# Attention scores of a two-layer trunk in fp32 pieces: the low query against both heads' high keys, the high query against high and low keys stacked in the rows, with halves moved between partitions by DMA

## The chip, the cores and the metric

The kernel runs on one core of one Trainium2 chip, in one launch. The metric is the device time of that launch in microseconds (us): 609.42 us, the median of 3 runs (609.11 to 610.04).

## What is computed

Two layers, each one RMSNorm, one wide input projection (1024 to 9808 columns, for 256 positions), three causal attention mixers of 8 heads of 64 (plain "a", indexer-selected "b", forgetting "c"), a SiLU gate per mixer, a projection per mixer, merge gates, an output projection and the residual; then one last norm. What the change touches is every product of queries and keys: the scores of the three mixers and those of the indexer.

```python
s_own = jnp.einsum('bhqd,bhkd->bhqk', qc, k_own).astype(jnp.float32) * scale      # a
rel = jax.nn.relu(jnp.einsum('bqhd,bsd->bqhs', qi, k_idx))                        # indexer: 8 query heads, one key
s = jnp.einsum('bqhd,bkhd->bhqk', qc, k)                                          # b and c, in chunks
p = jax.nn.softmax(s, axis=-1)
```

The 256 positions are one block of a, so a is plain causal attention. The indexer keeps 64 keys per query for b.

## The kernel before

**Numbers in two pieces.** TensorE multiplies `float32r` operands. To keep fp32 accuracy each fp32 operand X is split: ACT writes the high piece Xh (a copy rounded to `float32r`), DVE writes the low piece Xl = X - Xh. A product is then three matmuls that add up in one PSUM bank: high x high, low x high, high x low. Every weight goes through this: 1 MB or 0.5 MB chunks are loaded by the queue of SyncE (SP) into three `raw` buffers (L354), split by ACT into `wh` (L362) and by DVE into `wl` (L366), and multiplied (L410, all units of projections).

**Work units.** The PE's work is a list of units. A unit of the input projection (`unit_b`, L422) makes 128 output columns for all 256 positions: 24 matmuls of 256 moving columns. Units `q`, `k`, `g` of a pair of heads (128 rows = 2 heads of 64) make its query, key and gate; `m` units make merge gates, `y` units (12 matmuls) the projections of a finished mixer. `mixer` (L986) lists the units of a mixer, two pairs of heads at a time, in the order q, g, k; `between` (L997) puts m and y units among them as filling. `NB1` says how many of the merge-gate units of mixer b stand there and how many stand behind mixer b (L1040, L1042).

**The planner.** No engine's order is written by hand. Every step is given to `Plan.op` with its engine, an estimated cost, what it reads and writes, and a key (its unit's number, shifted). `Plan.run` (L138) then lists the steps: at each turn the engine that can start first takes, of its steps that are ready then, the one with the lowest key. Each engine, SP's queue among them, executes its list strictly in order. A step of SP that waits for its source so holds the loads listed behind it.

**Queries.** `ev_q` (L594): for a and b the projection is rotated first (`rope`, L461: DVE shuffle, POOL multiply, DVE multiply, POOL add; result `rr` in SBUF), for c it is read from PSUM. `split_to` (L390) writes `qh` by ACT and `ql` by DVE, 128 x 256 each; the rows are the two heads.

**Keys.** `ev_k` (L603) calls `write_bd` (L721). The key of the pair is stored block-diagonally, so that one matmul with all 128 rows serves both heads: tile `bd..h` is 128 x (2 x 256), head 0's key in the upper rows of the first half, head 1's in the lower rows of the second half, zeros elsewhere (written once, L912 to L919). `bd..l` is the same for the low piece. Per key that is two ACT copies (L727) and two DVE subtractions (L728), each on 64 rows. The indexer's one key (`ev_kwf`, L732) is written to both diagonal blocks.

**Scores.** `scores` (L574) is one step on PE. The queries are the stationary operand (128 positions at a time), the block-diagonal keys move: for the first 128 queries 2 x 128 key columns (only the causal part), for the second 128 queries 2 x 256.

```python
PE.matmul(o, qh[:, sl], mh, start=True, stop=False)     # L584
PE.matmul(o, ql[:, sl], mh, start=False, stop=False)    # L585
PE.matmul(o, qh[:, sl], ml, start=False, stop=True)     # L586
```

That is six matmuls per call: 3 of 256 columns and 3 of 512. `scores` is called 16 times per layer (12 pairs of the mixers by `attend`, L637; 4 pairs of the indexer by `index_scores`, L785), 32 times in all. The two heads' scores lie interleaved in PSUM (column, head), which the readers undo by a stride of 2 (L647, L797). After the scores come, per head and half: bias and row minimum (DVE, L647), exponential (ACT, L651), normalising, transposes (PE, L673), the split of the result (L676, L678) and the product with the values (PE, L690 to L693).

Of the kernel before, what the change touches and what calls it, by code (L numbers as in the profile page):

```python
# [47 lines left out]
NB1 = 0  # L48
# [186 lines left out]
def hybrid_trunk(ctx, tc, x, norm_gain, w_in, forget_bias, w_branch, w_out, final_gain, consts, out):  # L235
# [15 lines left out]
    def T(b):  # L251
        return b.slot[1]
# [29 lines left out]
    qs = [[pool.tile([128, S], F32R, name=f"q{p}{i}") for i in range(3)] for p in "hl"]  # L282
# [8 lines left out]
    bd = [[pool.tile([128, 2, S], F32R, name=f"bd{i}{p}") for p in "hl"] for i in range(NBD)]  # L291
# [41 lines left out]
    for nm, n, cols, dt in (("rsh", 2, S, F32), ("rr", 2, S, F32),  # L333
                            ("th", 2, S, F32), ("g", 4, S, F32), ("e", 4, 384, F32), ("st", 8, 8, F32),
                            ("fb", 2, 384, F32), ("ot", 2, S, F32), ("t8", 4, 8, F32), ("mth", MTH, S, F32)):
        tag(nm, n, [128, cols], dt)
# [134 lines left out]
    def new_bd():  # L471

        b = Buf("bd")
        return b, [[Tok(), Tok()], [Tok(), Tok()]]


# [97 lines left out]
    def scores(q, k, ktoks, key):  # L574
        s0, s1 = Buf("s"), Buf("s")
        kt = [t for h in ktoks for t in h]

        def go():
            qh, ql = T(q[0]), T(q[1])
            kh, kl = T(k)  # L580
            for o, sl, n in ((T(s0)[:, :256], slice(0, 128), 128), (T(s1), slice(128, 256), 256)):
                o = o.rearrange("p (c h) -> p c h", h=2)
                mh, ml = (x[:, :, :n].rearrange("p h c -> p c h") for x in (kh, kl))
                PE.matmul(o, qh[:, sl], mh, start=True, stop=False)  # L584
                PE.matmul(o, ql[:, sl], mh, start=False, stop=False)  # L585
                PE.matmul(o, qh[:, sl], ml, start=False, stop=True)  # L586
        pe(go, 3 * (t_mm(256) + t_mm(512)), [q[0], q[1], k] + kt, [s0, s1], key, "qk", MARGIN)
        return s0, s1

    class Pair:  # L590
# [3 lines left out]
        def ev_q(self, ps, key):  # L594
            q = self.q = (Buf("qh"), Buf("ql"))
            if self.mixer == "c":
                split_to(lambda: plain(T(q[0])), lambda: plain(T(q[1])), lambda: tiles(T(ps)[:, :S]), S, True, [ps], q[0], q[1],
                         key, -0.125, "q")
            else:
                r = rope(ps, "q", key)  # L600
                split_to(lambda: plain(T(q[0])), lambda: plain(T(q[1])), lambda: tiles(T(r)), S, False, [r], q[0], q[1], key, name="q")

        def ev_k(self, ps, key):  # L603
            self.k, self.kt = new_bd()
            src = ps if self.mixer == "c" else rope(ps, "k", key)
            write_bd(src, self.k, self.kt, key, self.mixer == "c")
# [30 lines left out]
        def attend(self, key):  # L637
# [3 lines left out]
            for h in range(2):  # L641
# [4 lines left out]
                for t, a, n, s in parts:  # L646
                    dve(lambda t=t, a=a, n=n, s=s, e=e, st=st, b=b, h=h: DVE.tensor_tensor_reduce(  # L647
                        T(e)[:, a:a + n], T(s)[:, :2 * n].rearrange("p (c h) -> p h c", h=2)[:, h], b()[:, a:a + n], 1.0, 3e38, ALU.add, ALU.min,
# [72 lines left out]
    def write_bd(src, b, toks, key, ps, shared=False):  # L721
        for h in range(2):
            o = slice(64 * h, 64 * h + 64)
            s = (lambda: tiles(T(src)[0:64, :S])) if shared else (lambda o=o: tiles(T(src)[o, :S]))
            hi = lambda o=o, h=h: plain(T(b)[0][o, h])
            lo = lambda o=o, h=h: plain(T(b)[1][o, h])
            act(lambda hi=hi, s=s: ACT.activation(hi(), s(), AF.Copy), S, ps, [src, k_bdz], [toks[h][0]], key, "bd", HALF + (0.0 if ps else 104.0), touch=[b])  # L727
            dve(lambda hi=hi, lo=lo, s=s: DVE.tensor_tensor(lo(), s(), hi().bitcast(F32), op=ALU.subtract), S,  # L728
                [src, toks[h][0]], [toks[h][1]], key, "bd", t_dve(S) + HALF + 15.0, touch=[b], port=not ps)


    def ev_kwf(l, ps, key):  # L732
        act(lambda: ACT.activation(plain(wf[64:80]), tiles(T(ps)[64:80, :S]), AF.Copy), S, True, [ps], [k_wf], key, "wf")
        b, toks = new_bd()
        write_bd(rope(ps, "k", key, 64), b, toks, key, False, shared=True)
        return b, toks
# [357 lines left out]
```

## Time and profile before

| | |
|---|---|
| median of 3 runs | 609.42 us |
| the profiled execution's own time | 609.16 us |
| its span, first to last instruction | 607.4 us |
| granted TensorE clock | 0.997 |
| DVE busy | 537.9 us (89%) |
| ACT busy | 406.8 us (67%) |
| POOL busy | 85.7 us (14%) |
| bytes moved by DMA | 105.55 MB, mean 174 GB/s |

A matmul's row gives its start and the time until its end, and matmuls overlap: the next one starts before the last has drained. How long PE is held by a matmul is therefore read from the distance between starts, not from the duration. PEld is the load of a stationary operand; it runs beside the matmul before it. In the timeline a row is: start, duration, engine, line, operation, out<-in, stationary rows*columns, moving rows x columns, count. In rows of one source line, three numbers with slashes are the shortest, median and longest duration in ns. An idle time in brackets names what ended it.

### The profile page before, as it was taken

The numbers are of one execution on the slowest core, as the hardware profiler recorded it, in microseconds if no ns is written. First come the engines' busy times: TensorE is split into PE (matmuls) and PEld (weight loads), VectorE is DVE, ScalarE is ACT, GpSimd is POOL, SyncE is SP. The second block draws the span as 40 slices with busy tenths as digits, with TensorE's granted clock in tenths as the row PEclk, the third lists the DMA queues.
The fourth block names the chain that finished last, engine by engine and source line by source line (L and its number), as shares of the span: only waits on it lengthen the run. The fifth ranks groups of instructions, "written<-read, shape, count | busy, mean of one in ns | idle before, by whom it ended". The sixth has DMA issues, their size and how long they took to land.

```text
span 607.4 us, 12561 instructions
## 1 busy us (share of the span) xinstructions
PE 599.1 (99%) x4856; PEld 580.8 (96%) x4856; DVE 537.9 (89%) x1270; ACT 406.8 (67%) x811; POOL 85.7 (14%) x100
## 2 busy tenths in 40 slices
PE   9999999999999999999999999999999999999995
PEld 8999999999999999999889999999999999999995
DVE  8799999887998999999588899978889989999883
ACT  6775487685776766785587554957767675859741
POOL 1224021100000222200003311201000004230001
PEclk9999999999999999999999999999999999999998
DMA  9866455837372562666555637474464437355801
GB/s 304 255 209 208 127 169 157 278 104 231 117 245 70 159 203 92 209 211 206 161 181 169 206 102 246 139 219 142 153 187 174 141 115 224 109 182 164 280 35 70
DMA packets 93853, 105.55 MB, mean 174 GB/s; under 512 B 4321, under 2 KB 82401, under 8 KB 93793
## 3 DMA queue, kind: packets, MB, share of 16 engines
q1 hardware_dynamic: 93504, 104.36, 53.8%
q8 instruction: 38, 0.62, 0.4%
q10 hardware_dynamic: 288, 0.39, 0.2%
q14 instruction: 23, 0.18, 0.1%
HBM read 103.69 MB, written 1.05 MB: 172 GB/s over the span
## 4 chain that ended last, share of the span: by engine, by line
PE 88%; DVE 9%; issue 1%; ACT 1%; DMA 0%; POOL 0%; POOLq 0%; DVEq 0%
PE proj L410 74%; DVE wl L366 3%; PE t L673 3%; PE proj L970 2%; PE s L586 2%; PE s L585 2%; PE s L584 2%; PE o L690 1%; PE o L693 1%; DVE isc L824 1%; DVE t L823 1%; PE t L629 1%; DVE isc L803 1%; DVE rsh L465 1%; PE o L692 0%
## 5 line engine op out<-in xcount | busy, mean ns | idle before, releaser
L366 DVE TENSOR_TENSOR wl<-raw,wh 128x1024 fp32r<-128x1024 f32 (+1 forms) x190 | 237.1, 1257 | 24.2 <-ACT wh L362 22.6
L362 ACT ACTIVATE wh<-raw 128x1024 fp32r<-128x1024 f32 (+1 forms) x190 | 198.6, 1058 | 74.3 <-PE proj L410 43.1
L410 PE MATMUL proj<-hTh,wh 128*128 128x256 f32 (+1 forms) x1040 | 246.4, 276 | 0.0
L410 PE MATMUL proj<-hTl,wh 128*128 128x256 f32 (+1 forms) x1040 | 245.6, 275 | 0.0
L410 PEld LDWEIGHTS proj<-hTl,wh 128*128 128x128 f32 (+1 forms) x1040 | 199.0, 191 | 0.4
L410 PEld LDWEIGHTS proj<-hTh,wh 128*128 128x128 f32 (+1 forms) x1040 | 198.9, 191 | 0.4
L410 PE MATMUL proj<-hTh,wl 128*128 128x256 f32 (+1 forms) x1040 | 160.1, 276 | 0.0
L410 PEld LDWEIGHTS proj<-hTh,wl 128*128 128x128 f32 (+1 forms) x1040 | 138.0, 191 | 0.9
L466 POOL TENSOR_TENSOR rsh<-rsh,cst 128x256 f32<-128x256 f32 (+1 forms) x42 | 33.0, 786 | 343.0 <-DVE rsh L465 333.9
L651 ACT ACTIVATE e<-e,st 128x128 f32<-128x128 f32 x96 | 42.6, 446 | 9.2 <-DVE st L647 8.9
L468 POOL TENSOR_TENSOR rr<-rr,rsh 128x256 f32<-128x256 f32 (+1 forms) x42 | 44.4, 1059 | 9.7 <-ACT wh L362 3.4
L410 PE MATMUL proj<-wh,v 128*128 128x512 f32 (+1 forms) x144 | 33.7, 356 | 0.0
L410 PE MATMUL proj<-og0l,wh 128*128 128x256 f32 x128 | 31.9, 275 | 0.0
L410 PE MATMUL proj<-og0h,wh 128*128 128x256 f32 x128 | 31.9, 275 | 0.0
L410 PE MATMUL proj<-wh,hTh 128*128 128x512 f32 x80 | 31.4, 393 | 0.0
L410 PE MATMUL proj<-wh,hTl 128*128 128x512 f32 x80 | 30.5, 382 | 0.2 <-DVE hTl L532 0.2
L706 ACT ACTIVATE ot<-o 64x256 f32<-64x256 f32 x48 | 18.3, 381 | 16.8 <-PE o L693 16.3
L410 PEld LDWEIGHTS proj<-wh,v 128*128 128x128 f32 x144 | 25.2, 190 | 2.9
L678 DVE TENSOR_TENSOR ptl<-t,pth 128x384 fp32r<-128x384 f32 x48 | 25.1, 551 | 0.2
L410 PE MATMUL proj<-og0h,wl 128*128 128x256 f32 x128 | 24.7, 275 | 0.0
L410 PEld LDWEIGHTS proj<-og0h,wh 128*128 128x128 f32 x128 | 24.6, 192 | 0.0
L410 PEld LDWEIGHTS proj<-og0l,wh 128*128 128x128 f32 x128 | 24.6, 192 | 0.0
(194 smaller groups left out, 1012.3 us busy)
## 6 DMA issues: line engine op xcount, KB each, us to landing
raw<-in_w_in_dram SPq DMA_DIRECT2D x74, 1024.0 KB, 5.2
raw<-in_w_branch_dram SPq DMA_DIRECT2D x24, 512.0 KB, 3.9
raw<-in_w_out_dram SPq DMA_DIRECT2D x8, 1024.0 KB, 5.5
raw<-in_w_in_dram SPq DMA_DIRECT2D x3, 512.0 KB, 6.3
x<-in_x_dram SPq DMA_DIRECT2D x4, 256.0 KB, 4.1
raw<-in_w_in_dram SPq DMA_DIRECT2D x2, 320.0 KB, 6.7
out_dram<-tmp SPq DMA_DIRECT2D x2, 320.0 KB, 2.5
raw<-in_w_in_dram SPq DMA_DIRECT2D x2, 256.0 KB, 3.4
```

The costliest lines, as they stand in the source:

```text
L362: ACT.activation(p[0].v, sel(c.v), AF.Copy)
L366: DVE.tensor_tensor(p[1].v, sel(c.v), p[0].v.bitcast(F32), op=ALU.subtract)
L410: PE.matmul(o(), a(), b(), start=first and i == 0, stop=last and i == n - 1)
L466: gps(lambda: POOL.tensor_tensor(T(sh)[:np_], T(sh)[:np_], s[:np_], op=ALU.mult), S, [k_rope], [sh], key, "rope")
L468: gps(lambda: POOL.tensor_tensor(T(r)[:np_], T(r)[:np_], T(sh)[:np_], op=ALU.add), S, [sh], [r], key, "rope")
L584: PE.matmul(o, qh[:, sl], mh, start=True, stop=False)
L585: PE.matmul(o, ql[:, sl], mh, start=False, stop=False)
L586: PE.matmul(o, qh[:, sl], ml, start=False, stop=True)
L651: act(lambda t=t, a=a, n=n, e=e, st=st: ACT.activation(T(e)[:, a:a + n], T(e)[:, a:a + n], AF.Exp, bias=T(st)[:, t:t + 1], scale=-1.0, acc ...
L673: PE.transpose(T(ps)[:, i * 128:(i + 1) * 128], T(es[h])[:, i * 128:(i + 1) * 128], ident)
L678: dve(lambda h=h, src=src: DVE.tensor_tensor(T(pl)[:, h], src(), T(ph)[:, h].bitcast(F32), op=ALU.subtract), 384, [ps, kp[h][0]], [kp[h][1 ...
L706: act(lambda r=r, h=h: ACT.activation(T(t)[r], T(o)[64:, h * S:(h + 1) * S], AF.Copy, scale=0.5), S, True, [o], [kt[h]], key, "og", HALF, ...
```

## The change

- **The products.** The block-diagonal tile now holds only the high key (`bd..h`). A second tile, `bd..e`, holds for each head the high key in that head's own 64 rows and the low key in the other 64 rows. The query's high piece is kept per head, once in the upper and once in the lower rows (`qh` is now 128 x (2 x 256)). One matmul of low query x block-diagonal high key serves both heads as before; then one matmul per head, with all 128 rows, adds high query x (high key + low key). Per half of the queries that is one matmul of 2n moving columns and two of n, in place of three of 2n (n = 128, 256). The half with n = 256 comes first.
- **The pieces.** ACT writes the high query and the high key twice side by side (512 columns in one instruction, reading the source twice). DVE makes the low query and the low key in one subtraction each on all 128 rows; the low key goes to a buffer `kl` of its own.
- **The moves.** What must change partitions goes by DMA on SP's queue (`move`, a new step): two transfers per query, four per key in two steps, each 64 rows x 256 columns (64 KB). A move is planned as 0.8 us of SP and landed 1.9 us later. The indexer's one key needs none: its two ACT copies, a third ACT copy and one DVE subtraction write all blocks.
- **Layout.** The scores of the two heads lie one behind the other in PSUM, no longer interleaved; the readers are changed to match.
- **Order.** `mixer` lists q, k, g in place of q, g, k. `NB1` is 2 in place of 0: two of the eight merge-gate units of mixer b stand among its pairs, six behind. There are 3 buffers `rr` in place of 2. Three zeroed tiles fall away. A smaller scratch area for DMA descriptors is asked for.

```diff
-NB1 = 0
+NB1 = 2
-    qs = [[pool.tile([128, S], F32R, name=f"q{p}{i}") for i in range(3)] for p in "hl"]
+    qs = [[pool.tile([128, 2, S] if p == "h" else [128, S], F32R, name=f"q{p}{i}") for i in range(3)] for p in "hl"]
+    klow = [pool.tile([128, S], F32R, name=f"kl{i}") for i in range(2)]
...
+    def move(dst, src, n, reads, writes, key, name, touch=()):
+
+        def go():
+            for d, a in zip(dst(), src()):
+                nc.sync.dma_start(d.bitcast(F32), a.bitcast(F32))
+        o = plan.op([("SP", 800.0, go)], reads, writes, key, 1900.0, name, touch)
+        o.margin = -1350.0
...
-            for o, sl, n in ((T(s0)[:, :256], slice(0, 128), 128), (T(s1), slice(128, 256), 256)):
-                o = o.rearrange("p (c h) -> p c h", h=2)
-                mh, ml = (x[:, :, :n].rearrange("p h c -> p c h") for x in (kh, kl))
-                PE.matmul(o, qh[:, sl], mh, start=True, stop=False)
-                PE.matmul(o, ql[:, sl], mh, start=False, stop=False)
-                PE.matmul(o, qh[:, sl], ml, start=False, stop=True)
+            for o, sl, n in ((T(s1), slice(128, 256), 256), (T(s0)[:, :256], slice(0, 128), 128)):
+                both = kh[:, :, :n].rearrange("p h (a b) -> p h b a", a=2)
+                PE.matmul(o.rearrange("p (h b a) -> p h b a", h=2, a=2), ql[:, sl], both, start=True, stop=False,
+                          skip_group_check=True)
+                for h in range(2):
+                    oh = o[:, h * n:(h + 1) * n].rearrange("p (b a) -> p b a", a=2)
+                    PE.matmul(oh, qh[:, h, sl], turns(ke[:, 0 if shared else h, :n]), start=False, stop=True,
+                              skip_group_check=True)
...
+    def split_q(q, src, ps, b, key, scale, name):
...
+        act(lambda: ACT.activation(T(q[0]).rearrange("p h (a b) -> p h a b", a=2), two(src()), AF.Copy, **sc), 2 * S, ps,
+            [b], [k], key, name, 0.0 if ps else 144.0, touch=[q[0]])
...
+        lo, up = slice(0, 64), slice(64, 128)
+        move(lambda: (T(q[0])[up, 0], T(q[0])[lo, 1]), lambda: (T(q[0])[lo, 0], T(q[0])[up, 1]), S, [], [q[0], k], key - 6, "dq")
...
+    def split_k(src, ps, key):
+        b, kl = Buf("bd"), Buf("klow")
...
+        act(lambda: ACT.activation(T(b)[1].rearrange("p h (a b) -> p h a b", a=2),
+                                   sv().unsqueeze(1).to_broadcast([128, 2, 2, 128]), AF.Copy), 2 * S, ps,
+            [src], [ka], key, "bd", 0.0 if ps else 144.0, touch=[b])
+        dve(lambda: DVE.tensor_tensor(plain(T(kl)), sv(), plain(T(b)[1][:, 0]).bitcast(F32), op=ALU.subtract), S,
+            [src, ka], [kl], key, "bd", t_dve(S) + (10.0 if ps else 26.0), touch=[b], port=not ps)
+        move(lambda: (T(b)[0][LO, 0], T(b)[0][UP, 1]), lambda: (T(b)[1][LO, 0], T(b)[1][UP, 1]), S, [ka, k_bdz], [k0],
+             key - 6, "dk", [b])
+        move(lambda: (T(b)[1][UP, 0], T(b)[1][LO, 1]), lambda: (T(kl)[LO], T(kl)[UP]), S, [kl], [ka, k1], key - 6, "dk", [b])
+        return b, [ka, k0, k1]
...
-                for hf in range(2) for kind in "qgk" for p in (2 * hf, 2 * hf + 1)]
+                for hf in range(2) for kind in "qkg" for p in (2 * hf, 2 * hf + 1)]
```

On PE, the scores of the first pair of mixer c in layer 0 stand so before (`s` are the two banks of scores, `bd2h` and `bd2l` the keys, `qh` and `ql` the queries, `proj` the unit around them):

```order
L410 MATMUL proj_158<-hTl,wh_68 128x256
L584 MATMUL s_159<-bd2h,qh_82 128x256
L585 MATMUL s_159<-bd2h,ql_85 128x256
L586 MATMUL s_159<-bd2l,qh_82 128x256
L584 MATMUL s_160<-bd2h,qh_82 128x512
L585 MATMUL s_160<-bd2h,ql_85 128x512
L586 MATMUL s_160<-bd2l,qh_82 128x512
L410 MATMUL proj_158<-hTh,wl_75 128x256 x4
```

The unit around them is the next pair's key (kc1). After the change the same scores stand as follows; the unit around them is now the next pair's gate (gc1), one key unit, two y units and one gate unit later:

```order
L412 MATMUL proj_160<-hTh,wl_74 128x256 x4
L586 MATMUL s_163<-bd2h,ql_85 128x512
L590 MATMUL s_163<-bd2e,qh_82 128x256 x2
L586 MATMUL s_162<-bd2h,ql_85 128x256
L590 MATMUL s_162<-bd2e,qh_82 128x128 x2
L412 MATMUL proj_160<-hTh,wh_68 128x256
```

There are still six matmuls. Between the last matmul of the key unit kc0 and these scores stand 20 matmuls of 256 columns and 4 small ones before, and 84 of 256 columns and 4 small ones now. Counted so for each of the 32 calls, from the last matmul of its query or key unit, the PE work in between is now least for the third pair of mixer c (kc2): 60 matmuls of 256 columns, 8 of the product with the values, 3 transposes and 4 small ones (20 and 4 small ones before).

On SP's queue, around the loads for the same stretch of mixer c in layer 0, there stand before only loads (`raw` are the three load buffers):

```order
L354 DMA raw_117<-in_w_in_dram 128x8x256
L354 DMA raw_115<-in_w_in_dram 128x8x256
L354 DMA raw_116<-in_w_branch_dram 128x4x256
L354 DMA raw_117<-in_w_in_dram 128x8x256
L354 DMA raw_115<-in_w_branch_dram 128x4x256
```

Now moves stand between them (`qh` a query's halves; `bd..h<-bd..e` the high key to the block-diagonal tile; `bd..e<-kl` the low key to the stacked tile; kc0's are those with `bd2`, kc1's those with `bd0`):

```order
L574 DMA qh_82<-qh_82 64x256 x2
L356 DMA raw_117<-in_w_in_dram 128x8x256
L574 DMA qh_80<-qh_80 64x256 x2
L574 DMA bd2h<-bd2e 64x256 x2
L356 DMA raw_118<-in_w_branch_dram 128x4x256
L574 DMA bd0h<-bd0e 64x256 x2
L574 DMA bd2e<-kl_86 64x256 x2
L356 DMA raw_119<-in_w_in_dram 128x8x256
L574 DMA bd0e<-kl_87 64x256 x2
```

Each load now has moves listed ahead of it and behind it. In all, SP's list grows from 124 transfers to 284: 160 moves, 64 for queries and 96 for keys.

More of the change, by code (lines that the diff above doesn't have):

```diff
@@ L290, in hybrid_trunk @@
     NBD = 3
-    bd = [[pool.tile([128, 2, S], F32R, name=f"bd{i}{p}") for p in "hl"] for i in range(NBD)]
+    bd = [[pool.tile([128, 2, S], F32R, name=f"bd{i}{p}") for p in "he"] for i in range(NBD)]
     pts = [pool.tile([128, 2, 384], F32R, name=f"pt{p}") for p in "hl"]
@@ L571, in final_norm, with scores @@
         plan.op([("SP", 50.0, lambda: nc.sync.dma_start(out_rows[:, B], tmp6[:, B]))], [ko[1], k_tmp[1]], [], key, 1900.0, "out")
-    def scores(q, k, ktoks, key):
+    def move(dst, src, n, reads, writes, key, name, touch=()):
[4 more added lines that the diff above has]
+        o.margin = -1350.0
+    def scores(q, k, ktoks, key, shared=False):
@@ new lines, in scores @@
+        pe(go, 775.0, [q[0], q[1], k] + ktoks, [s0, s1], key, "qk", MARGIN)
+        return s0, s1
+    def split_q(q, src, ps, b, key, scale, name):
+        k = Tok()
+        two = lambda x: x.unsqueeze(1).to_broadcast([128, 2, 2, 128])
+        sc = {} if scale is None else {"scale": scale}
+        act(lambda: ACT.activation(T(q[0]).rearrange("p h (a b) -> p h a b", a=2), two(src()), AF.Copy, **sc), 2 * S, ps,
+            [b], [k], key, name, 0.0 if ps else 144.0, touch=[q[0]])
+        hi = lambda: plain(T(q[0])[:, 0]).bitcast(F32)
+        if scale is None:
+            f = lambda: DVE.tensor_tensor(plain(T(q[1])), src(), hi(), op=ALU.subtract)
+        else:
+            f = lambda: DVE.scalar_tensor_tensor(plain(T(q[1])), src(), scale, hi(), op0=ALU.mult, op1=ALU.subtract)
+        dve(f, S, [b, k], [q[1]], key, name, t_dve(S) + (10.0 if ps else 26.0), touch=[q[0]], port=not ps)
+        lo, up = slice(0, 64), slice(64, 128)
+        move(lambda: (T(q[0])[up, 0], T(q[0])[lo, 1]), lambda: (T(q[0])[lo, 0], T(q[0])[up, 1]), S, [], [q[0], k], key - 6, "dq")
@@ L719, in gated @@
                      k_og[self.oi][0][self.p], k_og[self.oi][1][self.p], key, name="og")
[L721 to L729, printed above, removed]
+    LO, UP = slice(0, 64), slice(64, 128)
@@ L732, in ev_kwf @@
     def ev_kwf(l, ps, key):
         act(lambda: ACT.activation(plain(wf[64:80]), tiles(T(ps)[64:80, :S]), AF.Copy), S, True, [ps], [k_wf], key, "wf")
-        b, toks = new_bd()
-        write_bd(rope(ps, "k", key, 64), b, toks, key, False, shared=True)
-        return b, toks
+        r, b = rope(ps, "k", key, 64), Buf("bd")
+        ka, k0, k1 = Tok(), Tok(), Tok()
+        sv = lambda: tiles(T(r)[LO, :S])
+        for o, h, k in ((LO, 0, k0), (UP, 1, k1)):
+            act(lambda o=o, h=h: ACT.activation(plain(T(b)[0][o, h]), sv(), AF.Copy), S, False, [r, k_bdz], [k], key, "bd",
+                HALF + 104.0, touch=[b])
@@ L738, in wf_cols @@
+        act(lambda: ACT.activation(plain(T(b)[1][LO, 0]), sv(), AF.Copy), S, False, [r], [ka], key, "bd", HALF + 104.0, touch=[b])
+        dve(lambda: DVE.tensor_tensor(plain(T(b)[1][UP, 0]), sv(), plain(T(b)[1][LO, 0]).bitcast(F32), op=ALU.subtract), S,
+            [r], [ka], key, "bd", t_dve(S) + HALF + 15.0, touch=[b], port=True)
+        return b, [ka, k0, k1]
     def wf_cols(l, key):
@@ L912, in hybrid_trunk @@
     for b in bd:
-        for t in b:
+        for t in b[:1]:
             z = t.rearrange("p h c -> p (h c)")
```

36 lines of the change are left out of this document (17 added, 19 removed).

## The prediction

> **What bounds the kernel now.** I read the page first, then PE's waits, the chain of waits, and the timeline at one call of the scores.
>
> ```profile
> span 607.4 us, 12561 instructions
> PE 599.1 (99%) x4856; PEld 580.8 (96%) x4856; DVE 537.9 (89%) x1270; ACT 406.8 (67%) x811; POOL 85.7 (14%) x100
> PE 88%; DVE 9%; issue 1%; ACT 1%; DMA 0%; POOL 0%; POOLq 0%; DVEq 0%
> PE t L885 <- DVE ones L881: 1.1, 1, 1.1
> PE s L586 <- DVE bd2l L728: 0.5, 1, 0.5
> PE proj L410 <- DVE hTl L532: 0.2, 1, 0.2
> ```
>
> PE is busy 599.1 of 607.4 us, it makes 88% of the chain that ended last, and its waits come to 1.8 us, 1.1 of them before the first matmul. Busy time alone would not prove that PE sets the time, since matmuls overlap; the chain and the absence of waits do. So a change of the PE work goes into the time nearly one for one, as long as what PE needs is still there when it arrives.
>
> How long one matmul holds PE is read from starts. Two pieces of the chain are runs of equal matmuls without a break (start, duration, count): 256 columns at L410, 512 columns at L970.
>
> ```profile
> 49.51 8.04 PE proj L410 x72
> 15.01 6.48 PE proj L970 x30
> ```
>
> 8.04 / 72 = 0.1117 us for 256 columns, 6.48 / 30 = 0.216 us for 512. The call of the scores that the order shows (first pair of mixer c, layer 0) stands in PE's timeline so:
>
> ```profile
> 153.86 0.28 PE L584 MATMUL s<-bd2h,qh 128*128 128x256 f32 x1
> 153.97 0.28 PE L585 MATMUL s<-bd2h,ql 128*128 128x256 f32 x1
> 154.08 0.28 PE L586 MATMUL s<-bd2l,qh 128*128 128x256 f32 x1
> 154.20 0.38 PE L584 MATMUL s<-bd2h,qh 128*128 128x512 f32 x1
> 154.41 0.38 PE L585 MATMUL s<-bd2h,ql 128*128 128x512 f32 x1
> 154.63 0.38 PE L586 MATMUL s<-bd2l,qh 128*128 128x512 f32 x1
> 154.85 0.61 PE L410 MATMUL proj<-hTh,wl 128*128 128x256 f32 x4
> ```
>
> From the first to the matmul behind them it is 154.85 - 153.86 = 0.99 us; by the two rates, 3 x 0.1117 + 3 x 0.216 = 0.983 us. The call runs at full rate.
>
> **The products.** The new call has one matmul of 512 columns, three of 256 and two of 128. The first four cost 0.216 + 3 x 0.1117 = 0.551 us. What the two of 128 columns cost is the open price, because the next matmul's stationary operand has to be loaded meanwhile. Two groups of rows bound it.
>
> ```profile
> 37.46 0.37 PE L778 MATMUL t<-fz,cst 128*128 128x8 f32 x2
> 37.68 0.37 PE L779 MATMUL t<-fz,ones 128*128 128x8 f32 x2
> 37.91 0.36 PE L584 MATMUL s<-bd0h,qh 128*128 128x256 f32 x1
> ...
> 201.08 0.22 PE L691 MATMUL o<-pth,v 128*128 128x128 f32 x1
> 201.14 0.22 PE L692 MATMUL o<-ptl,v 128*64 128x128 f32 x1
> 201.20 0.28 PE L693 MATMUL o<-ptl,v 128*64 128x256 f32 x1
> ```
>
> Upper end: four matmuls with only 8 moving columns, each followed by one with 128 stationary columns, take 37.91 - 37.46 = 0.45 us, 0.112 each. With 8 columns to move, the length must come from something else, and a load of 128 stationary columns per matmul is what they share. Lower end: L691 and L692 move 128 columns each and take 0.06 us each (201.08, 201.14, 201.20), but behind both comes a load of only 64 stationary columns (128*64). In the new call both 128-column matmuls are followed by a load of 128 columns: the second head's query, then the next unit's weights. That is the first group's case, so I take 0.112: the call costs 0.551 + 2 x 0.112 = 0.775 us, a gain of 0.983 - 0.775 = 0.208 us. For 32 calls that is **6.7 us**. At the lower end, 0.551 + 0.12 = 0.671 us per call, the gain is 0.312 x 32 = 10.0 us.
>
> [...]
>
> No other matmul is removed or added; order and NB1 only move units.
>
> **The split on ACT and DVE.** These feed PE and lie beside it.
>
> ```profile
> L728 DVE TENSOR_TENSOR bd1l<-rr,bd1h x14: 422/453/873, 78.8 to 552.0; 64x256 fp32r<-64x256 f32 x14
> L728 DVE TENSOR_TENSOR bd1l<-proj,bd1h x4: 406/422/428, 179.5 to 455.4; 64x256 fp32r<-64x256 f32 x4
> ...
> L401 DVE SCALAR_TENSOR_TENSOR v<-acc,v 128x256 fp32r<-128x256 f32 x16 | 6.9, 461 | 0.0
> L793 ACT ACTIVATE tmp<-s 128x512 f32<-128x512 f32 x8 | 4.7, 593 | 0.5 <-PE s L586 0.5
> L396 ACT ACTIVATE qh<-rr 128x256 fp32r<-128x256 f32 x24 | 11.5, 480 | 0.2 <-POOL rr L468 0.2
> ```
>
> A subtraction on 64 rows takes 0.42 to 0.45 us, one of the same length on 128 rows 0.46: rows are free, so each of 24 keys saves one, about 0.45 x 24 = 11 us of DVE. ACT: a query's copy goes from 0.48 (256 columns) to about 0.6 to 0.75 (512; the row from PSUM has 0.593), a key's two copies become one such; over 32 queries and 24 keys a few us either way. Neither engine bounds, so this is worth nothing by itself; it can only shorten rare late operands. The worst of those is the wait of 0.5 us above (PE s for bd2l). I count it as 0.3 us of gain, bounds 0 and 0.7 (the two waits behind the start).
>
> **The moves.** 160 transfers of 64 KB are added. Rows for the issue on SP and for the time from issue to landing:
>
> ```profile
> L354 SPq DMA_DIRECT2D raw<-in_w_in_dram x76: 367/368/502, 6.2 to 543.2; - x76
> ...
> raw<-in_w_in_dram SPq DMA_DIRECT2D x74, 1024.0 KB, 5.2
> raw<-in_w_branch_dram SPq DMA_DIRECT2D x24, 512.0 KB, 3.9
> ...
> out_dram<-tmp SPq DMA_DIRECT2D x2, 320.0 KB, 2.5
> ```
>
> Nothing here copies from SBUF to SBUF. The nearest rows say 2.5 us for a transfer with nothing else in the queue (out, 320 KB) and 5.2 us for one that shares it with a load; a move behind a load should land with that load or just after it. The shortest chain is that of mixer c's keys (no rotation): ACT 0.6, DVE 0.46, the issues ahead of the low key's landing 4 x 0.37 = 1.5 (the next pair's high key stands before it), landing 2.5 to 5.2: 5.1 to 7.8 us, plus 0.2 or so per hop between engines. Against it stands the PE work between key unit and scores: for kc0 84 x 0.1117 + 4 x 0.112 = 9.8 us; for kc2, the least, 60 x 0.1117 = 6.7 and about 1.4 for the rest, 8.1 us. So the moves are covered, in the worst place by little. If that cover is gone, the whole lateness goes into the time, call by call. I charge 0.5 us for a few late ones; bounds 0 and 6 us (0.2 us at each of 32).
>
> What else is queued behind the moves: loads. A move that waits for its source on SP delays the next load. Loads have room:
>
> ```profile
> SPq L354 <- DVE wl L366: 409.0, 75, 13.3
> DMA  9866455837372562666555637474464437355801
> ```
>
> SP spends 409 us waiting for a load buffer to come free, and the DMA engines are 50 to 60% busy after the first 30 us; the moves add 160 x 0.37 = 59 us of SP and 10.5 MB to 105.55. I price that at zero; PE has no wait on a weight now.
>
> **The sum**, against the profiled execution's own time of 609.16 us (span 607.4; the median of the runs is 609.42, 0.26 more): 609.16 - 6.7 - 0.3 + 0.5 = **602.7 us**. Its own range, from the bounds of the small terms, is 601 to 604.5.
>
> **The rivals.** *The 128-column matmuls cost 0.06 us* (the L691 rows, if the load can be taken further ahead than the 8-column rows suggest): 609.16 - 10.0 = 599.2 us. Against it: in the L691 rows the load was half as wide. Chance 0.1.
>
> *Late moves eat part of the gain.* The planner's fixed 1.9 us for a landing is below every row (2.5 to 5.2); its queue model makes up for a load ahead of a move, perhaps not for several. With 0.05 to 0.15 us lost per call, 1.6 to 4.8 us, the time is 604 to 607.5. For it: PE is in order and a call that waits stops everything. Against: cover of 8 us and more. Chance 0.13.
>
> *Slower: SP becomes the place where PE's operands wait.* Mechanism: a move stands in SP's list behind a load that waits for its buffer (the 409 us above, up to 13.3 at a time), so the high query lands only after a `wl` subtraction far down DVE's list; PE then idles at the scores. It decides from 6.7 / 32 = 0.21 us per call on. If a quarter of the calls (8) lost 1.5 us each, 12 us, the time would be 609.16 - 6.7 + 12 = 614 us. For it: DVE is nearly full where the indexer's selection runs, so buffers come free late there.
>
> ```profile
> 350.00:400.00 50.00, 49.38 (x439) 48.81 (x438) 49.42 (x143) 33.00 (x63) 9.54 (x12) 1.00 0.55 170
> ```
>
> DVE has 49.42 of 50 us there, and PE already misses 0.6. Against it: the change takes DVE work out of exactly this, and the order keeps moves ahead of later loads. Chance 0.07, and 0.05 for losses that just cancel the gain (608.2 to 610.4). That the change does not do what it says can be excluded: the order shows the six new matmuls per call.
>
> **How the numbers follow.** The forecast case has 0.65. A measurement of this kernel can tell about 0.2%, 1.2 us, from no change. Faster by more than that: 0.65 + 0.1 + 0.13 = 0.88; within it 0.05; slower 0.07. The range leaves out the slower cases and the cancelled gain, 0.12 together, and otherwise reaches from the cheap 128-column matmul less a little relief, 599.0, to the middle of the late-move case, 606.0.
>
> **What would show it.** In the profile after: the scores' six matmuls take 0.775 us from the first start to the matmul behind them (0.67 for the first rival); 128-column starts lie 0.112 apart; PE's waits name no DMA, or by under 1 us; the span is 600 to 602. It is wrong if PE waits for a DMA of `qh` or `bd` at several calls by tenths of a us, if SP's waits show moves held behind a full load buffer, or if weights (`wh`, `wl`) appear among PE's waits.

## The result, and the profile after

The changed kernel takes **613.73 us** (median of 15 runs, 610.75 to 615.53) against 609.36 us for the kernel before (15 runs, 609.11 to 610.04): ratio 1.0067, 95% interval 1.0052 to 1.0082. It is slower by 0.7%. The profiled execution took 615.29 us, near the slow end of this spread. The prediction had 602.7 us, in 599.0 to 606.0.

The page of the changed kernel answers the first rows of the prediction:

```profile
span 613.5 us, 12883 instructions
PE 598.6 (98%) x4856; PEld 579.3 (94%) x4856; DVE 532.7 (87%) x1252; ACT 409.1 (67%) x779; POOL 85.6 (14%) x96
PE 73%; DVE 13%; DMA 6%; ACT 3%; issue 2%; SPq 1%; POOL 0%; POOLq 0%; DVEq 0%; ACTq 0%
```

PE's share of the chain that ended last fell from 88 to 73%, and transfers, which had no part in it, now hold 6%. PE's busy time looks unchanged (599.1 before), although its work became shorter (592.2 busy in the run without moves, below): part of the waits, and a stretch at half clock, are counted in it. PE's waits name the place (time in all, count, longest):

```profile
PE s L590 <- DMA bd1e<-kl: 2.1, 2, 1.0
PE s L590 <- issue: 1.9, 2, 1.7
PE s L590 <- DMA bd0h<-bd0e: 1.1, 1, 1.1
```

All three stand at L590, the new matmuls of high query x (high + low key). First, a call that waits for nothing, in PE's timeline:

```profile
451.17 0.38 PE L586 MATMUL s<-bd0h,ql 128*128 128x512 f32 x1
451.39 0.38 PE L590 MATMUL s<-bd0e,qh 128*128 128x256 f32 x2
451.61 0.28 PE L586 MATMUL s<-bd0h,ql 128*128 128x256 f32 x1
451.72 0.33 PE L590 MATMUL s<-bd0e,qh 128*128 128x128 f32 x2
451.89 0.33 PE L412 MATMUL proj<-hTh,wh 128*128 128x256 f32 x1
452.05 0.28 PE L412 MATMUL proj<-hTl,wh 128*128 128x256 f32 x1
452.17 0.28 PE L412 MATMUL proj<-hTh,wh 128*128 128x256 f32 x1
```

From first start to the matmul behind, the call takes 451.89 - 451.17 = 0.72 us. But the next distance is 0.16 instead of 0.112. The stationary loads (PEld) of this stretch start 0.11 us apart (451.61, 451.72, 451.83, 451.94, 452.06), while the matmul behind the first short one starts after 0.058 (451.72, 451.78); so the 0.05 us gained there on the pace of the loads comes back in the 0.16. Measured to the sixth matmul behind, less five times 0.1117, the call costs 0.774 us (median of 30 calls of the trace), against 0.982 before (23 calls). The gain on PE is 0.208 us a call, 6.7 us in all, to the digit what was forecast.

Now a call that waits: the third pair of mixer c in layer 1, the kind of place that the prediction called the worst covered. ACT's and DVE's timeline for its key, then SP's queue, then PE:

```profile
467.23 0.60 ACT L745 ACTIVATE bd2e<-proj 128x512 fp32r<-128x512 f32 x1
...
468.02 0.42 DVE L748 TENSOR_TENSOR kl<-proj,bd2e 128x256 fp32r<-128x256 f32 x1
...
466.73 2.39 SPq L574 DMA_DIRECT2D qh<-qh  x2
469.22 1.19 SPq L574 DMA_DIRECT2D bd2h<-bd2e  x2
470.50 0.54 SPq L356 DMA_DIRECT2D raw<-in_w_in_dram  x1
471.13 1.13 SPq L574 DMA_DIRECT2D bd2e<-kl  x2
...
475.11 0.38 PE L586 MATMUL s<-bd2h,ql 128*128 128x512 f32 x1
476.63 0.66 PE L590 MATMUL s<-bd2e,qh 128*128 128x256 f32 x2 [1.13 <-DMA bd0h<-bd0e]
```

The low key is ready at 468.44, while SP still stands in the last of the query moves, until 469.12. The low key's two transfers are issued from 471.13 and 471.67 on, behind the high key's and behind a load of 1 MB at 470.50. That load lands at 476.32, the two transfers at 476.58 and 476.87; PE starts L590 at 476.63, 1.3 us later than without a wait (0.22 us behind L586's start). (The bracket names another transfer of the same queue, still to land; the matmul needs `bd2e`.) Each move's issue takes about 0.55 us of SP (median), not the 0.37 of a load before. The landings of the whole run (count, KB each, median us from issue):

```profile
raw<-in_w_in_dram SPq DMA_DIRECT2D x74, 1024.0 KB, 5.8
raw<-in_w_branch_dram SPq DMA_DIRECT2D x24, 512.0 KB, 5.6
...
qh<-qh SPq DMA_DIRECT2D x64, 64.0 KB, 2.0
...
bd1e<-kl SPq DMA_DIRECT2D x16, 64.0 KB, 5.7
```

A low key's 64 KB land almost as late as 1 MB (5.7 us here, 4.7 in the other two tiles). Sorted by the loads still in flight when the issue ended: 75 moves with no load took 2.0 us (median), 70 with one load 4.2, 14 with two 6.2, one with three 8.0. Of the 85 that had a load in flight, all 85 landed after the last of those loads, by 0.5 us (median). Eight calls of the scores come late in this profile. At every one it is the low key's move, issued with a load in flight, and the matmul of L590 that needs it starts 0.04 to 0.14 us after the move has landed.

The longest wait ends at 521.51, 0.09 us after the first half of its low key had landed; by the measure used above L590 is 1.89 us late there. It has a second price. The matmul's row, in which the profile names no releaser, then PE and the others by stretches of the span (length, PE, PEld, DVE, ACT, POOL busy with counts, granted clock, DMA share, GB/s):

```profile
521.51 0.69 PE L590 MATMUL s<-bd1e,qh 128*128 128x256 f32 x2 [1.73 <-issue]
...
515.00:519.00 4.00, 4.00 (x38) 4.00 (x38) 3.78 (x6) 2.20 (x4) 0.00 (x0) 1.00 0.96 296
519.00:522.60 3.60, 1.87 (x15) 1.45 (x14) 0.33 (x1) 1.06 (x1) 0.00 (x0) 1.00 1.09 292
522.60:526.10 3.50, 3.50 (x19) 3.50 (x18) 2.52 (x12) 2.37 (x10) 0.00 (x0) 0.51 1.05 320
```

The DMA engines are full through all three stretches (share 0.96, 1.09 and 1.05), and in the last PE makes 19 matmuls at half clock (0.51) where full clock makes some 33 (38 in 4.00 us in the first): the low clock lasts 3.41 us (522.62 to 526.03) and costs 1.7.

### The profile page after: what moved, and what is told of

Its sections match the earlier page's. It is cut to its first block, busy times and chain, and to the rows that moved or that the text cites. A ratio compares the mean times of both kernels' runs of the same rounds, so it can differ in the third digit from the quotient of the medians.

```text
span 613.5 us, 12883 instructions
## 1 busy us (share of the span) xinstructions
PE 598.6 (98%) x4856; PEld 579.3 (94%) x4856; DVE 532.7 (87%) x1252; ACT 409.1 (67%) x779; POOL 85.6 (14%) x96
## 3 DMA queue, kind: packets, MB, share of 16 engines
HBM read 103.69 MB, written 1.05 MB: 171 GB/s over the span
## 4 chain that ended last, share of the span: by engine, by line
PE 73%; DVE 13%; DMA 6%; ACT 3%; issue 2%; SPq 1%; POOL 0%; POOLq 0%; DVEq 0%; ACTq 0%
PE proj L412 63%; DVE wl L368 5%; DMA raw<-in_w_in_dram 3%; PE t L691 2%; PE s L590 2%; DMA bd1e<-kl 2%; PE proj L1002 1%; ACT wh L364 1%; PE s L586 1%; DVE isc L856 1%; DVE t L855 1%; DMA x<-in_x_dram 1%; DVE rsh L467 1%; DMA bd0h<-bd0e 1%; PE o L711 1%
## 5 line engine op out<-in xcount | busy, mean ns | idle before, releaser
L468 POOL TENSOR_TENSOR rsh<-rsh,cst 128x256 f32<-128x256 f32 (+1 forms) x42 | 34.3, 818 | 385.0 <-DVE rsh L467 346.1
L470 POOL TENSOR_TENSOR rr<-rr,rsh 128x256 f32<-128x256 f32 (+1 forms) x42 | 46.3, 1108 | 6.9 <-DVE rr L469 4.0
L691 PE MATMUL t<-cst,e 128*128 128x128 f32 x144 | 23.7, 276 | 0.8 <-DVE e L679 0.7
```

The lines of the kernel that those rows point to most:

```text
L468: gps(lambda: POOL.tensor_tensor(T(sh)[:np_], T(sh)[:np_], s[:np_], op=ALU.mult), S, [k_rope], [sh], key, "rope")
L470: gps(lambda: POOL.tensor_tensor(T(r)[:np_], T(r)[:np_], T(sh)[:np_], op=ALU.add), S, [sh], [r], key, "rope")
L691: PE.transpose(T(ps)[:, i * 128:(i + 1) * 128], T(es[h])[:, i * 128:(i + 1) * 128], ident)
```

## The experiments

Theory A: the moves land behind the loads issued just ahead of them, PE waits for them at the scores, and the clock falls behind the longest wait. Theory B: the loss is in the new order of the blocks and in late work of ACT and DVE.

### No moves, same order

```diff
-                nc.sync.dma_start(d.bitcast(F32), a.bitcast(F32))
+                pass
```

> The same lists of PE, ACT, DVE and POOL as the changed kernel, but SP issues none of the 160 moves (so the scores are formed from halves that were not exchanged). Theory A (the moves land behind the 1 MB loads that SP issued just before them, PE waits for them at the scores, and its clock falls after the longest wait): all waits of PE at the scores for a DMA go, 8.0 us in the profile, and the 1.6 us of slow clock behind one of them; 601 to 604 us. Theory B (the time was lost in the new order, or in ACT and DVE work that comes late): the waits stay in other places; 608 us or more.

602.57 us (602.31 to 602.73), ratio 0.9885 (0.987 to 0.99).

```profile
span 600.5 us, 12518 instructions
PE 592.2 (99%) x4856; PEld 576.4 (96%) x4856; DVE 531.9 (89%) x1252; ACT 408.6 (68%) x779; POOL 85.6 (14%) x96
```

No DMA is among PE's waits. So the moves cost 613.73 - 602.57 = **11.2 us**, and everything else together is worth 602.57 - 609.36 = -6.8 us, which is PE's 6.7 and no more. Where the two profiles (spans 613.5 and 600.5) part, matmul by matmul (PE's order is the same in both): 8.1 us at eight calls of the scores (0.32, 0.37, 1.49, 0.53, 1.40, 1.57, 2.19, 0.21), 1.7 us of half clock, and about 2.3 us net at five other places, whose cause stays open. The last 0.9 us of the 13 arose in the first 12 us, before the first move was issued at 37.67, and is not the moves'.

### The same, with small loads

Every `dma_start` of a weight after the first six carries one row block:

```diff
+            first = len(chunks) <= 6
...
-                nc.sync.dma_start(c.v, ap)
+                nc.sync.dma_start(*((c.v, ap) if first else (c.v[:, :1], ap[:, :1])))
```

> The changed kernel in its own order with its moves by DMA; every weight load after the first six chunks is still issued at its place with its waits, but carries one of its 4 or 8 row blocks, so most of the weights' bytes are left out. Theory A: with little data ahead of them the moves land about 2 us after their issue, as those did that had no load outstanding, the waits of the scores for a DMA go (8 us and the low clock behind the longest of them, 1.6 us), 601 to 605 us. Rival A2 (the moves are late because SP issues them late, behind waits of its own and at 0.55 us each): the issues stand at the same places in SP's queue behind the same buffer waits, so the scores' waits stay, 609 us or more. Theory B (order and engines): nothing that it blames is changed, 611 to 614 us.

602.44 us (602.23 to 603.7), ratio 0.989 (0.9876 to 0.9904). Page and landings:

```profile
span 600.5 us, 12874 instructions
PE 592.1 (99%) x4856; PEld 576.2 (96%) x4856; DVE 531.8 (89%) x1252; ACT 409.2 (68%) x779; POOL 85.5 (14%) x96
```

```profile
raw<-in_w_in_dram SPq DMA_DIRECT2D x59, 128.0 KB, 2.3
...
qh<-qh SPq DMA_DIRECT2D x64, 64.0 KB, 2.0
...
bd1e<-kl SPq DMA_DIRECT2D x16, 64.0 KB, 2.1
```

All 160 moves are there, at the same places of SP's list, with waits for their sources that are no shorter (the row for `ql` has 99.6 us in 18 waits, 78.2 in 18 in the changed kernel) and issues of 0.55 us; most of the bytes ahead of them are gone (25.68 MB read from HBM in place of 103.69), and the time is that of the kernel without moves. This settles the cause: not the moves' issue, not SP's order as such, not the engines, but the data queued ahead.

### The order alone

The kernel before, with blocks q, k, g and `NB1` 2.

```diff
-NB1 = 0
+NB1 = 2
...
-                for hf in range(2) for kind in "qgk" for p in (2 * hf, 2 * hf + 1)]
+                for hf in range(2) for kind in "qkg" for p in (2 * hf, 2 * hf + 1)]
```

> The kernel before with only the two order changes: units in the order q, k, g, and two merge-gate units of mixer b among its pairs. Theory A: no PE work changes and nothing waits for a DMA at the scores, so 608.5 to 611 us. Theory B: most of the loss is here, 612 us or more.

613.49 us (613.33 to 613.74), ratio 1.0065 (1.005 to 1.008): 4.0 us above the 609.50 us of the kernel before in the same series. Theory A's 608.5 to 611 us missed, and theory B's 612 or more came. The first of PE's waits:

```profile
PE proj L410 <- DVE rr L467: 2.2, 2, 1.1
```

A bank of `proj` is held by a rotation that is late, for 2.2 of the 4.0 us. The kernel before has two buffers `rr` and the changed one three, and its calls and splits are longer, so this run does not price the order within the change; the two runs above do, where the same order stands and nothing of it is lost. It shows that the order may not be called free without the rest.

### Moves on ACT's queue

```diff
-                nc.sync.dma_start(d.bitcast(F32), a.bitcast(F32))
-        o = plan.op([("SP", 800.0, go)], reads, writes, key, 1900.0, name, touch)
-        o.margin = -1350.0
+                nc.scalar.dma_start(d.bitcast(F32), a.bitcast(F32))
+        plan.op([("ACT", 800.0, go)], reads, writes, key, 1900.0, name, touch)
```

> The changed kernel with the moves issued by ACT, so on a queue of their own beside the loads; the planner charges ACT 0.8 us per move of two transfers. Theory A in its narrow form (it is the place behind a load in the same queue that makes a move late): moves land about 2 to 3.5 us after issue whether a load is under way or not, PE's waits at the scores fall under 2 us, 602 to 606 us, unless ACT's 64 to 90 us more of issuing delays the weights. Theory A in its wide form (the 16 DMA engines are simply busy with the load): landings stay at 4 us and more while a load is under way, 609 us or more.

643.44 us (642.35 to 648.48), ratio 1.0572 (1.053 to 1.0614). A row of the landings, then PE's waits:

```profile
bd1e<-kl ACTq DMA_DIRECT2D x16, 64.0 KB, 4.5
```

```profile
PE s L589 <- DMA bd1e<-kl: 5.2, 4, 2.9
PE s L589 <- DMA bd2e<-kl: 5.1, 5, 1.6
```

The moves now have a queue without loads, and still land late: with no load in flight 2.0 us, with one 4.2, as before, and 110 of 127 land after the last load. On top, the issues take 91 us of ACT, another 12 to 15 us go by while ACT stands at moves whose operands are not ready, and four stretches of low clock follow (mean clock 0.987, 0.995 in the changed kernel; from 85.70 to 89.10 it is 0.50); how the 30 us above the changed kernel divide between these stays open. The narrow form of theory A is refuted, the wide form had this side: the queue of the issuing engine is not where the loads go ahead. By what way loads in flight hold a move back was not shown: the landings are read from semaphores, and no run separates when the data of a move arrived from when its semaphore did.

### A later landing in the plan

The planner's 1900 ns from a move's issue to its landing set to 5000, and to 3000.

> The changed kernel, but the planner is told that a move lands 5.0 us after SP is done with it in place of 1.9 us: nothing is issued otherwise, the scores are only listed later on PE, behind more of the other units. Theory A: the moves are as late as before, but PE has other work; the waits at the scores fall under 2 us and the clock stays full: 602 to 606 us. Theory B: no change beyond 1 us.

> The changed kernel with the planner told that a move takes 3.0 us to land in place of 1.9 (5.0 was tried in the late plan). Theory A: some of the scores' waits for a DMA go, those for moves behind one load that land 6 to 8 us after the issue stay; the units that the planner puts in front take less from what keeps the end of a mixer fed than at 5.0: 606 to 612 us. Theory B: as the late plan, 612 to 614 us.

With 5000: 612.33 us (610.69 to 613.8), ratio 1.0042 (1.0027 to 1.0057). With 3000: 613.46 us (611.59 to 615.85), ratio 1.0066 (1.0045 to 1.0088). Both missed what theory A expected (602 to 606 and 606 to 612 us); with 3000 theory B's 612 to 614 came, with 5000 the change is 1.4 us, where theory B allowed 1. Yet the scores' waits went, as theory A has it: none for a DMA is left in either profile. But the units put in front of the scores are missing elsewhere; the first of PE's waits with 5000, and with 3000:

```profile
PE proj L412 <- ACT og0h L398: 3.3, 1, 3.3
```

```profile
PE proj L412 <- ACT og0h L398: 4.6, 2, 2.4
```

At the end of mixer b only `y` units are left, and these need the last pair's result, which now comes later; in each profile one stretch of low clock follows (with 5000 from 573.15 to 576.56, 3.41 us at 0.50; with 3000 in the slice from 274.7 to 289.9 us, the only one of the page's 40 below 0.9). The lateness was moved, not removed.

### Moves ahead of loads in SP's queue

Only SP's list is changed: a load planned within 4.5 us (6 us) ahead of a move is put behind it.

```diff
+        if o.name in ("dq", "dk"):
+            held, i = [], len(out) - 1
+            while i >= 0 and out[i][1] >= t - HOP:
...
+            out.append(m)
+            out += held
```

> The changed kernel; PE, ACT, DVE and POOL keep its order row for row. Only SP's queue differs: a load that the plan issues within 4.5 us ahead of a move is issued behind it. Theory A: a move then finds at most an older load in flight, lands some 2 to 4 us after its issue, and most of the 8 us of the scores' waits goes; the loads start 1 to 3 us later, which costs where a piece of weights was just in time, 0 to 3 us in all: 603 to 608 us. Rival (the loads have no room, so what the moves gain the weights lose): waits of PE for wl and wh of the same size take their place, 611 us or more.

> As the one before, with 6 us for 4.5. Theory A: within 2 us of it, lower if loads that were issued 4.5 to 6 us ahead still held moves back, higher if later loads cost: 602 to 609 us. Rival: more waits for weights than with 4.5 us, 612 us or more.

**684.49 us** (679.52 to 687.05), ratio 1.1218 (1.1179 to 1.1257), and 708.21 us, ratio 1.1593 (1.1572 to 1.1613): the rival's side, and far beyond the 611 and 612 us from which it began. SP's, ACT's and PE's waits with 4.5 us:

```profile
SPq L380 <- DVE wl L392: 155.6, 33, 13.8
SPq L598 <- DVE ql L627: 125.0, 18, 15.0
...
ACT wh L388 <- DMA raw<-in_w_in_dram: 95.5, 25, 7.0
...
PE t L715 <- DVE e L703: 26.1, 10, 7.6
```

The moves do land sooner (97 instead of 75 find no load in flight). But SP stands 125 us at query moves, which wait for the subtraction of `ql` that still reads their tile (78.2 in the changed kernel), loads behind them start late, ACT waits 95.5 us for them in its own list (32.4), and everything that ACT and DVE have listed behind those splits is late: the normalised `e` by up to 7.6 us. The rival had looked for waits of PE for `wl` and `wh` themselves; 2.7 us of these came, and the rest reached PE through `e` and its like. 37.5 us at half clock (mean clock 0.971) are part of the loss with 4.5 us. So SP's long waits for a buffer were not room: a move put there waits for its own operands and holds the loads behind it.

### Engine copies in place of moves

`move` becomes two copies of 64 x 256 on ACT or DVE, as the planner likes; once in the changed order, once in the old one (q, g, k, `NB1` 0).

```diff
+                ACT.activation(d, a.bitcast(F32), AF.Copy)
...
+                DVE.tensor_copy(d, a.bitcast(F32))
...
-        o = plan.op([("SP", 800.0, go)], reads, writes, key, 1900.0, name, touch)
...
+        plan.op([("ACT", 1000.0, on_act), ("DVE", 600.0, on_dve)], reads, writes, key + 6, 0.0, name, touch).port = True
```

> The moves are made by ACT or DVE copies from one partition half to the other, 64x256 each, two a move, where the planner puts them; no DMA carries them and SP issues loads alone. The block order and NB1 are the changed kernel's. Theory A (what costs is that a moved half lands only behind the loads issued before it): the score calls keep their shorter time, the loads land as in the kernel before, and what is added is some 85 moves of two copies, each about 0.3 to 0.5 us, 50 to 85 us of busy time on engines that have 74 and 198 us free: 602 to 606 us, and no wait of the scores for a DMA. Theory B (the loss is in the order of the blocks and the room that ACT and DVE have for it): this adds work to the engines that are late already, so 612 to 620 us, with waits for DVE and ACT in place of those for the DMA.

> As the kernel with engine copies, with the block order q, g, k and NB1 0 of the kernel before. Theory A has the order matter little: within 1.5 us of the kernel with engine copies in the changed order, on either side; with less room between k and the scores the copies may be late at some calls, 0.2 to 0.5 us each for up to 8 calls, so 603 to 608 us. Theory B (the new order by itself costs some 4 us, as the run of the order alone had it): 4 us below the kernel with engine copies in the changed order, about 600 us.

613.03 us (612.54 to 614.26), ratio 1.006 (1.0048 to 1.0072), and 615.7 us (614.65 to 618.48), ratio 1.011 (1.0091 to 1.013). DVE goes from 532.7 to 549.6 us busy, ACT from 409.1 to 439.2, and PE waits for them: 2.7 us for `wl` and 1.7 for `bd1h` in the first. The first time is on theory B's side, by its second half: the added work makes ACT and DVE late. In the old order the time is 2.7 us worse, where theory A expected 603 to 608 us and theory B 600; both missed.

### Keys written where they belong

DVE forms the low key in two subtractions of 64 rows, each written straight to the other half of the partitions, in place of one of 128 rows and a move; in the second kernel ACT also writes the blocks' high keys, and only queries move.

```diff
+        half = lambda o, i, h: DVE.tensor_tensor(plain(T(b)[1][o, h]), tiles(T(src)[i, :S]), plain(T(b)[1][i, h]).bitcast(F32),
+                                                 op=ALU.subtract)
+        for o, i, h in ((UP, LO, 0), (LO, UP, 1)):
...
```

> The low halves of the keys are written straight to the other partition half by two DVE subtractions of 64x256 in place of one of 128x256 and a move; the high halves of the keys and of the queries still move by DMA. 64 of the 160 DMAs of moves go, DVE gets 32 more instructions of about 0.35 us (11 us; it has 74 us free). Theory A (a moved half lands behind the loads): all but one of the scores' waits for a DMA were for the low keys, so most of the 8 us and the low clock behind the longest go; what stays are waits for high keys of some 1 us at a few calls, and the planner's new order may be late elsewhere by 1 to 3 us: 603 to 608 us, so faster than the kernel before. Theory B (the room of DVE): with DVE's 11 us more and a new order, late at e, wl and og by as much as was saved, 609 us or more.

> As the one before, and ACT writes the high keys of the blocks itself in two activations of 64x256, so only the queries' halves move by DMA (64 of 160 DMAs). ACT gets 64 more instructions of about 0.3 to 0.4 us, 20 to 25 us; it has 200 us free. Theory A: no wait of the scores for a DMA of keys; 602 to 607 us, unless ACT's extra 0.7 us ahead of each k delays the low halves that DVE forms from what ACT wrote. Theory B: ACT and DVE are late as with the engine copies of all moves (613 us), 609 to 615 us.

619.18 us (617.32 to 620.17), ratio 1.0159 (1.0142 to 1.0175), and 610.9 us (610.53 to 612.42), ratio 1.003 (1.0018 to 1.0041). Both missed theory A's ranges (603 to 608 and 602 to 607) and lie on theory B's side. In the first, the new list has DVE late with `e` (3.2 us, and low clock behind it, in the slice of the page from 492.4 to 507.8 us), a high key still lands 1.3 us late, and smaller pieces follow; where the rest of its time went stays open. In the second no wait for a DMA of keys is left, but three rows of a new kind, at four places:

```profile
PE proj L410 <- DVE bd0e L746: 2.1, 2, 1.1
PE proj L410 <- DVE bd2e L746: 1.1, 1, 1.1
PE proj L410 <- DVE bd1e L746: 1.0, 1, 1.0
```

DVE's timeline shows why the bank is held: the halves of a key stand behind the previous pair's row minima (L663), and the second behind a reciprocal as well.

```profile
177.24 0.42 DVE L663 CUSTOM_DVE_ANT_0 e<-s,fb 128x256 f32<-128x256 f32 x1
177.59 0.08 DVE L663 DVE_READ_ACCUMULATOR2_ANT st<- 128x1 f32 x1
177.70 0.42 DVE L746 TENSOR_TENSOR bd2e<-proj,bd2e 64x256 fp32r<-64x256 f32 x1
178.15 0.17 DVE L670 RECIPROCAL st<-st 128x2 f32<-128x2 f32 x1
178.35 0.43 DVE L746 TENSOR_TENSOR bd2e<-proj,bd2e 64x256 fp32r<-64x256 f32 x1
```

### The halves first, and the fastest kernel

The low halves get a key 10 lower; then ACT's high keys are read from SBUF, so that the bank is free sooner; then the same in the old order.

```diff
-            dve(lambda o=o, i=i, h=h: half(o, i, h), S, [src, ka], [k1[h]], key, "bd", t_dve(S) + HALF + (0.0 if ps else 15.0),
+            dve(lambda o=o, i=i, h=h: half(o, i, h), S, [src, ka], [k1[h]], key - 10, "bd", t_dve(S) + HALF + (0.0 if ps else 15.0),
```

> As the keys written directly, with DVE's low halves of a key ahead of other DVE work that is ready at the same time (the previous pair's maxima among it). Work and bytes are unchanged. If place is what costs (theory C): the proj banks come free about 1 us sooner at six places, 5 to 6 us less, 604 to 607 us, faster than the kernel before. If it is the room of ACT and DVE (theory B): the maxima are late in their place, and the scores' banks or e with them, 609 to 613 us.

> As the one before, and ACT copies the high keys of the blocks from SBUF instead of PSUM, some 0.1 us longer each, 6 us of ACT in all, but the proj bank is held by two instructions less. Theory C: as the one before or up to 1 us faster, 603 to 607 us. Theory B: 609 to 613 us.

> As the one before, with blocks in the order q, g, k and NB1 0 as in the kernel before. A pair's keys now have no gate block between them and the scores, and all that stands there is engines' work of about 2 us. If the changed order is needed to cover it, 2 to 4 us slower than the one before; if the order costs by itself (4 us in the run of the order alone), up to 3 us faster: 602 to 610 us.

608.51 us (608.22 to 609.09), ratio 0.9986 (0.9977 to 0.9995); **607.09 us** (606.96 to 607.97), ratio 0.9966 (0.9953 to 0.9979); and 607.61 us (605.68 to 611.3), ratio 0.9975 (0.996 to 0.9991). The second beats both kernels, the one before by 2.3 us. Its page and waits:

```profile
span 605.3 us, 12736 instructions
PE 593.6 (98%) x4856; PEld 576.4 (95%) x4856; DVE 534.8 (88%) x1251; ACT 433.5 (72%) x849; POOL 87.3 (14%) x99
```

```profile
PE proj L410 <- DVE rr L467: 1.3, 2, 0.6
...
PE proj L410 <- DVE wl L366: 0.9, 2, 0.6
PE t L645 <- DVE ptl L694: 0.7, 2, 0.3
```

With the work unchanged, the place alone gave 610.9 - 608.51 = 2.4 us, under half of the 5 to 6 that theory C expected, so that the time fell between the two theories' ranges; the second kernel came out at the upper end of theory C's range. The old order is not different from the new one here by more than the runs spread. Against the 602.57 us without moves, 4.5 us are still missing: 2.9 of them stand in the three waits for DVE shown, the rest stays open.

## Why the prediction was wrong

- **PE sets the time, and the call goes from 0.983 to 0.775 us: right.** 0.982 and 0.774 were measured, and the kernel without moves is faster by 6.8 us for 6.7 forecast. Its sign was looked for in the wrong place: the starts of the 128-column matmuls lie 0.058 us apart, as in the rival's rows, and the rest, up to the 0.11 us at which the stationary loads start, shows in the 0.165 behind the next one. Whoever had stopped at the 0.72 us would have credited the change with 8.4.
- **"So the moves are covered, in the worst place by little", charged at 0.5 us with bounds 0 and 6: this step failed.** The moves cost 11.2 us. The cover was right: in the call shown PE came about 8 us after the key's copy began (467.23 to 475.33, where L590 would have started), as forecast for kc2 (8.1). The chain was not 5.1 to 7.8 us but 9.6 (467.23 to 476.87): 2.7 us from the low key to its first issue, where 4 x 0.37 was allowed for all issues, since SP stood in a query move for the first 0.7 of them, a move's issue takes 0.55 and a load's issue stands between; then 5.5 and 5.2 us of landing. With some four hops of 0.2 (ACT's copy ends at 467.83, DVE starts at 468.02) the forecast chain itself reached about 8.6 us at its upper end, over the cover of 8.1; that overlap was answered with 0.5 us. The prediction's own sentence, "a move behind a load should land with that load or just after it", was exactly what happened, 85 times in 85, and the landing then is that of the load, which itself became later (5.2 to 5.8 us). Nor was kc2 the only place: over all 24 keys of pairs, from the copy on, the chain took 5.9 to 11.2 us against a cover of 6.3 to 13.6, and the eight late calls are those whose chain was longer than their cover; two of the eight are kc2. The two keys with the least cover, 6.3 us, were in time, since their moves found no load in flight. What decides is the load ahead, not the cover alone.
- **The range of the sum** does not follow from its own bounds: 609.16 - 6.7, with 0 to 0.7 of gain and 0 to 6 of loss, is 601.8 to 608.5, not 601 to 604.5. The bound of 6 us itself was too small.
- **The low clock** behind the wait of 1.89 us, 1.7 us, was not in the sum at all.
- **"Loads have room", priced at zero: wrong as a reading,** though it cost nothing here: weights stand among PE's waits in the changed kernel with 0.2 us. SP's 409 us of waits for buffers were taken for slack. Listing the loads of the last 4.5 or 6 us behind the moves cost 71 to 94 us.
- **DVE and ACT, 0.3 us of gain:** cannot be told. The wait for `bd2l` is gone, but the 6.8 us of the kernel without moves leave 0.1 for it. DVE's busy time fell by 5.2 us, not 11, since the planner places other work anew: ten of the normalisations of `e`, for one, went from ACT to DVE.
- **Order and `NB1` at nothing:** borne out within the change (602.57 us), not by themselves (4.0 us slower in the kernel before).
- **The rivals.** The case "late moves" had the mechanism and spread it thin, 0.05 to 0.15 us on every call; it is eight calls with 0.2 to 2.2 us. The slower rival, chance 0.07, gave 614 us by 8 calls of 1.5 us, and 613.7 with eight late calls came. That the number fits is partly luck: the eight calls lost 8.1 us and not 12, and the low clock and the other places made up for it. Its place was half right: SP's queue is where it happens, but not by a load that waits for its buffer. In the call shown the load had been issued without a wait; what held the move was the load's data.

## What to carry to other kernels

Price a small transfer not by its size but by the bytes in flight when it is issued: here 2.0 us alone, and otherwise the landing of the last load ahead plus 0.5. Add up its whole chain from the source's first instruction to landing, issues included, and set that against the cover call by call; where chain and cover overlap in range, the charge is the overlap, not a token. A queue's long wait for its turn is not room for work that has to wait itself: used as room, it cost 71 and 94 us here. And where engines are 88% full, the place of an instruction in their lists counts beside its length: 2.4 us here for the same work at another place.

## What the runs showed of the hardware

- On one queue, 418 of 418 moves that had loads in flight landed after the last of them (the changed kernel 85, later landing in the plan 113 and 98, moves ahead of loads 63 and 59); from another engine's queue, 110 of 127.
- The stretches of half clock that were read one by one: 3.41 us in the changed kernel (522.62 to 526.03), 3.41 us with a later landing of 5000 (573.15 to 576.56), and clock 0.50 from 85.70 to 89.10 with the moves on ACT's queue. In the traces of the two kernels the points at which the granted clock changes lie whole multiples of 3.413 us apart: 175 of them before (5.86 to 603.20), 151, 1 and 25 after (7.21, 522.62, 526.03, 611.37). In the changed kernel the pause of 1.89 us at 521.51 was followed by half clock; pauses of 1.2 to 1.3 us (ending at 180.07, 412.92 and 476.63) were not. The length of a pause does not decide alone: in the run with 3000 half clock followed the pause from 271.86 to 274.22 and none the pause from 570.66 to 572.89. What else decides was not shown.
- In the changed kernel's calls a matmul of 128 columns starts its follower after 0.058 us even when the next stationary load is 128 wide; the missing time is paid one matmul later (0.165 in place of 0.112).
- An SBUF-to-SBUF transfer of 64 rows takes 0.55 us of SP to issue, where the loads before took 0.37.
